# Transposes of rotated q and k, of the softmax and of the gated q and k: squares of 32 on VectorE and GpSimd transfers in place of TensorE

## The chip, the cores and the metric

The kernel runs on one core of a Trainium2 chip. The metric is the device time of one execution in microseconds (us), smaller is better. The time before is 1736.4 us, the median of three runs (1735.93 to 1738.6).

## The reference

One decoder layer on a sequence of 256 tokens of width 2048, in float32: a gated feed-forward block (FFN), a mixer of two kinds of attention, and a second FFN. Cut to what matters here:

```
x = x + 0.5 * swiglu(rms_norm(x, g1), w_gate1, w_up1, w_down1)
h = rms_norm(x, g_mix)
q_g, k_g, v_g, g_low, r_g, q_a, k_a, v_a = split(h @ w_in)
# group A: gated linear attention, 4 heads, chunks of 64 positions
b = cumsum(log_a) per chunk           # log_a from g_low
o_g = intra(q_g*exp(b-b_ref), k_g*exp(b_ref-b), v_g) + inter(q_g*exp(b), k_g*exp(b_last-b), v_g)
# group B: dilated attention, 8 heads of 128
qa, ka = rope(rms_norm(q_a)), rope(rms_norm(k_a))
o_a = softmax over three dilated causal windows (qa ka^T) v_a
x = x + concat(rms_norm(o_g) * silu(r_g), o_a) @ w_out
x = x + 0.5 * swiglu(rms_norm(x, g2), w_gate2, w_up2, w_down2)
```

## The kernel before, in words

Tokens lie on partitions in two tiles of 128 (t = 0, 1; `NT` is 2). Every large product is made of float32r matmuls of 128x512 on TensorE. To keep float32 accuracy a weight tile is split into a high part `wh` (ScalarE, L113) and a low part `wl` (VectorE, L114), and three products are added up: high by high (L274), low by high (L276), high by low (L278). A weight tile is 128x1024, and serves 12 such matmuls. `wh` and `wl` have four buffers each (`WBUF`), so the two engines that split can run a few tiles ahead of TensorE and no more.

`column_pair` makes 1024 columns of one projection: 16 weight tiles, for both token tiles, then an evacuation from PSUM by ScalarE (`store` for q, k, v). The mixer runs the pairs in the order q, k, v of the dilated attention, the low-rank gate (`gate_low`, 32 matmuls of 128x256, two weight tiles whose free columns GpSimd clears at L203), q and k of the linear attention (`qg`, `kg`), its v, its output gate, and then the output projection. The small work of the attention itself is put into the list `later` as closures, and each pair runs that list off between its own products: head work of q is done while k's products run, and so on. Tile then schedules all instructions with its own model of the engines, and that decides in which order each engine gets them. An engine works through its queue strictly in this order.

What the change touches:

- `rotate` (L596) normalizes and rotates 128x512 of q or k (four heads) on VectorE into `m1`; four TensorE transposes (L109) put it into a PSUM bank, and ScalarE copies that into `qT` or `kT` (L610). It runs 8 times.
- `scores` (L639) makes the scores of one head from `qT` and `kT` (L642) in a bank from `tp_bank`, adds the mask (L645), takes the softmax (L649 to L654) into `sc`. `values` (L657) transposes three blocks of `sc` on TensorE, copies them to `pT` on ScalarE (L663), and multiplies with v (L666 to L668) into another bank; `split` writes the output as `oah` (ScalarE) and `oal` (VectorE). 8 heads each.
- `scaled` (L730) transposes `qg` and `kg`, 128x512 per token tile, on TensorE, and VectorE multiplies the bank with the decays `e1`, `e2`, `e3` (L736).
- `tp_bank` (L80) has two banks only, taken in rotation by transposes, scores, values and the small products of the linear attention.
- `squares` (L126) and `move_squares` (L130) are there already, and the FFN uses them: one VectorE instruction transposes each square of 32x32 in place of its own, and 16 GpSimd transfers then carry the squares to the partitions where they belong. All GpSimd transfers go through one queue in order, with GpSimd's other work.

Of the kernel before, what the change touches and what calls it, by code (L numbers as in the profile page):

```python
# [14 lines left out]
F32 = mybir.dt.float32  # L15
# [33 lines left out]
def layer_kernel(tc, x, xT, gains, gla_gate_up, gla_gate_bias, gla_out_norm, att_q_norm, att_k_norm,  # L49
# [6 lines left out]
    with ExitStack() as es:  # L56
# [69 lines left out]
        def squares(dst, src):  # L126

            nc.vector.transpose(dst.rearrange("p (q j c) -> p j q c", q=4, j=4), src)

        def move_squares(dst, src):  # L130
            for q in range(4):
                for r in range(4):
                    nc.gpsimd.dma_start(dst[32 * q:32 * q + 32, r * P:(r + 1) * P], src[32 * r:32 * r + 32, q * P:(q + 1) * P])  # L133
# [406 lines left out]
        with tc.tile_pool(name="mix", bufs=1, reuse_waits="tile") as mp:  # L540
# [55 lines left out]
            def rotate(i, dst, t, half, xn):  # L596
                rs = head_scale(xn, 4, HD)
# [9 lines left out]
                tb = tp_bank()  # L607
                for h in range(4):
                    transpose(tb[:, h * P:(h + 1) * P], m1[:, h * P:(h + 1) * P])
                nc.scalar.activation(dst[:, 4 * half:4 * half + 4, t * P:(t + 1) * P], v(tb), AF.Copy)  # L610

            def store(dst, after=None):

                def f(t, ps):
                    for j in range(2):
                        blk = dst[:, t, j * 512:(j + 1) * 512]
                        nc.scalar.activation(halves(blk), ps[j], AF.Copy, scale=rt[:, t:t + 1])
                        if after:
                            later.append(lambda blk=blk, j=j: after(t, j, blk))
# [4 lines left out]


            xq, qT = big("xq"), big("qT")
            qTv = qT.rearrange("p (h s) -> p h s", h=AH)
            column_pair(hacts, store(tok(xq), lambda t, j, b: rotate(0, qTv, t, j, b)), span=14, due=8)
            xk, kT = big("xk"), big("kT")
            kTv = kT.rearrange("p (h s) -> p h s", h=AH)  # L630
            column_pair(hacts, store(tok(xk), lambda t, j, b: rotate(1, kTv, t, j, b)))
# [7 lines left out]
            def scores(h):  # L639
                b = tp_bank()  # L640
                for t in range(NT):
                    nc.tensor.matmul(b[:, t * P:t * P + (t + 1) * P], lhsT=qTv[:, h, t * P:(t + 1) * P],  # L642
                                     rhs=kTv[:, h, :(t + 1) * P], start=True, stop=True)
# [11 lines left out]
                heads[h] = sc  # L655

            def values(h):  # L657
                sc = heads.pop(h)
                tb = tp_bank()
                for j in range(3):  # L660
                    transpose(tb[:, j * P:(j + 1) * P], sc[:, j * P:(j + 1) * P])
                pT = mp.tile([P, 3 * P], F32, name="pT", tag="sc", bufs=6)
                nc.scalar.activation(pT, tb[:, :3 * P], AF.Copy)  # L663
                ob = tp_bank()
                v0, v1 = (vav[:, t, h * HD:(h + 1) * HD] for t in range(NT))
                nc.tensor.matmul(ob[:, 0:P], lhsT=v0, rhs=pT[:, 0:P], start=True, stop=True)  # L666
                nc.tensor.matmul(ob[:, P:S], lhsT=v0, rhs=pT[:, P:2 * P], start=True, stop=False)
# [9 lines left out]
            for h in range(0, AH, 2):  # L677
                later.append(lambda h=h: both(scores, h))
                if h:
                    later.append(lambda h=h: both(values, h - 2))  # L680
# [235 lines left out]
```

## Time and profile before

| | us |
|---|---|
| median of 3 runs | 1736.4 |
| the profiled execution | 1736.26 |
| its span in the trace | 1734.5 |
| TensorE (PE) busy | 1725.2 |
| VectorE (DVE) busy | 1299.5 |
| ScalarE (ACT) busy | 921.3 |
| GpSimd (POOL) busy | 438.9 |

The profile is of one execution. Its span is 1.8 us shorter than the time of the same execution, and that time is 0.14 us below the median. "Busy" counts an instruction from its start to its end; instructions of one engine overlap at their ends, so the distance between two starts is shorter than a duration. Times in the text count from the start of the span.

### The profile page before, as it was taken

The page shows a single profiled execution, that of the slowest core. Times are in us where ns is not written, and L with a number is a line of the kernel's source. Part 1 is how long each engine was busy: PE and PEld are TensorE (multiplying, and loading weights), DVE is VectorE, ACT ScalarE, POOL GpSimd, SP SyncE. Part 2 cuts the span into 40 slices and gives each one's busy share as a digit, 9 for nine tenths or more (in the row PEclk, how much of TensorE's full clock was granted, in tenths as well). Part 3 has the DMA queues.
Part 4 walks back from the last instruction along what each step waited for, and adds up shares of the span by engine and source line. Part 5 has one row for each costly group of instructions (what it writes and reads, how often), then busy time and mean ns, then how long its engine had stood idle before and what let it go on. Part 6 is the DMA issues. An engine that isn't in the chain of part 4 may idle for free.

```text
span 1734.5 us, 22127 instructions
## 1 busy us (share of the span) xinstructions
PE 1725.2 (99%) x8100; PEld 1503.4 (87%) x8100; DVE 1299.5 (75%) x1535; ACT 921.3 (53%) x1142; POOL 438.9 (25%) x870
## 2 busy tenths in 40 slices
PE   9999999999999999999999999999999999999999
PEld 7888888888888888888888888888888888888887
DVE  7788888855788787566655658688888965687875
ACT  7555555544555554565754545455555544455453
POOL 0333334444300601011000033333333343320000
PEclk9999999999999999999999999999999999999999
DMA  8666566666656656555444465556666666655653
GB/s 341 219 221 228 207 215 224 234 221 220 209 201 222 209 216 241 194 195 210 161 170 161 155 207 186 226 209 234 224 225 223 219 216 223 209 211 210 232 213 137
DMA packets 80846, 367.59 MB, mean 212 GB/s; under 512 B 19249, under 2 KB 36657, under 8 KB 38497
## 3 DMA queue, kind: packets, MB, share of 16 engines
q1 hardware_dynamic: 50864, 350.25, 55.9%
q0 software_dynamic: 29152, 14.87, 3.4%
q8 instruction: 63, 1.03, 0.2%
q10 hardware_dynamic: 720, 1.07, 0.2%
q14 instruction: 47, 0.38, 0.1%
HBM read 350.38 MB, written 2.10 MB: 203 GB/s over the span
## 4 chain that ended last, share of the span: by engine, by line
PE 82%; DVE 9%; DMA 5%; issue 2%; ACT 1%; POOL 1%; SPq 0%; DVEq 0%; ACTq 0%
PE acc L276 20%; PE acc L278 20%; PE acc L274 20%; DVE wl L114 4%; DMA raw<-in_w_ff_dram 4%; PE tp L278 3%; PE tp L276 3%; PE tp L274 3%; PE acc L300 2%; PE acc L299 2%; PE acc L298 2%; ACT wh L113 1%; DVE raw L246 1%; DMA urs<-us 1%; DVE t L238 1%
## 5 line engine op out<-in xcount | busy, mean ns | idle before, releaser
L114 DVE TENSOR_TENSOR wl<-raw,wh 128x1024 fp32r<-128x1024 f32 (+1 forms) x658 | 793.3, 1218 | 302.9 <-ACT wh L113 299.4
L113 ACT ACTIVATE wh<-raw 128x1024 fp32r<-128x1024 f32 (+1 forms) x660 | 682.2, 1048 | 562.5 <-PE acc L278 337.0
L133 POOL DMA_DIRECT2D urs<-us x704 | 344.3, 497 | 551.9 <-issue 287.6
L276 PE MATMUL acc<-wl,hh 128*128 128x512 f32 x1376 | 416.6, 381 | 0.4 <-DVE wl L114 0.4
L278 PE MATMUL acc<-wh,hl 128*128 128x512 f32 x1376 | 414.6, 380 | 0.0
L274 PE MATMUL acc<-wh,hh 128*128 128x512 f32 x1376 | 409.2, 381 | 1.6 <-ACT wh L113 1.6
L274 PEld LDWEIGHTS acc<-wh,hh 128*128 128x128 f32 x1376 | 259.5, 189 | 39.3 <-ACT wh L113 2.7
L276 PEld LDWEIGHTS acc<-wl,hh 128*128 128x128 f32 x1376 | 259.4, 189 | 38.6 <-DVE wl L114 1.5
L278 PEld LDWEIGHTS acc<-wh,hl 128*128 128x128 f32 x1376 | 259.6, 189 | 36.5
L276 PE MATMUL acc<-wl,uh 128*128 128x512 f32 x408 | 122.8, 379 | 0.0
L278 PE MATMUL acc<-wh,ul 128*128 128x512 f32 x408 | 122.5, 379 | 0.0
L274 PE MATMUL acc<-wh,uh 128*128 128x512 f32 x408 | 119.6, 379 | 0.2 <-ACT wh L113 0.2
L133 POOL DMA_DIRECT2D hh<-us x128 | 62.2, 508 | 158.9 <-issue 133.5
L274 PEld LDWEIGHTS acc<-wh,uh 128*128 128x128 f32 x408 | 77.0, 189 | 11.6 <-ACT wh L113 0.6
L278 PEld LDWEIGHTS acc<-wh,ul 128*128 128x128 f32 x408 | 77.1, 189 | 11.0
L276 PEld LDWEIGHTS acc<-wl,uh 128*128 128x128 f32 x408 | 77.1, 189 | 10.9
L165 POOL TENSOR_TENSOR rs<-a,mhalf 128x4 f32<-128x4 f32 (+1 forms) x12 | 17.4, 1454 | 256.8 <-DVE a L592 256.8
L274 PE MATMUL tp<-wh,hh 128*128 128x512 f32 x192 | 58.6, 379 | 0.0
L278 PE MATMUL tp<-wh,hl 128*128 128x512 f32 x192 | 57.1, 379 | 0.0
L276 PE MATMUL tp<-wl,hh 128*128 128x512 f32 x192 | 57.1, 379 | 0.0
L238 DVE TENSOR_TENSOR t<-raw 128x1024 f32<-128x1024 f32 x28 | 33.8, 1207 | 25.6 <-DMA raw<-in_w_ff_dram 25.6
L113 ACT ACTIVATE wh<-t 128x1024 fp32r<-128x1024 f32 x28 | 29.5, 1054 | 39.7 <-DVE t L238 33.0
(273 smaller groups left out, 1994.8 us busy)
## 6 DMA issues: line engine op xcount, KB each, us to landing
raw<-in_w_ff_dram SPq DMA_DIRECT2D x175, 1024.0 KB, 5.0
raw<-in_w_dn_dram SPq DMA_DIRECT2D x88, 1024.0 KB, 4.8
raw<-in_w_mix_dram SPq DMA_DIRECT2D x48, 1024.0 KB, 4.7
raw<-in_w_out_dram SPq DMA_DIRECT2D x16, 1024.0 KB, 4.8
urs<-us POOLq DMA_DIRECT2D x704, 16.0 KB, 3.6
xs<-in_x_dram SPq DMA_DIRECT2D x2, 1024.0 KB, 9.7
hh<-us POOLq DMA_DIRECT2D x128, 16.0 KB, 3.4
xt<-in_xT_dram SPq DMA_DIRECT2D x7, 256.0 KB, 6.6
```

The source lines that it names most:

```text
L113: nc.scalar.activation(dst_h, src, AF.Copy)
L114: nc.vector.tensor_sub(dst_l, src, dst_h.bitcast(F32))
L133: nc.gpsimd.dma_start(dst[32 * q:32 * q + 32, r * P:(r + 1) * P], src[32 * r:32 * r + 32, q * P:(q + 1) * P])
L165: nc.gpsimd.tensor_tensor(dst, src, mhalf[:, :src.shape[-1]], op=ALU.pow)
L238: nc.vector.tensor_add(room["sum"], b1, mid)
L246: nc.vector.tensor_add(raw[:, 1, j, :], b, raw[:, 1, j, :])
L274: nc.tensor.matmul(ps[j], lhsT=sh, rhs=alt(wh[:, j, :]), start=first and i == 0, stop=False)
L276: nc.tensor.matmul(ps[j], lhsT=sh, rhs=alt(wl[:, j, :]), start=False, stop=False)
L278: nc.tensor.matmul(ps[j], lhsT=sl, rhs=alt(wh[:, j, :]), start=False, stop=last and i == len(ws) - 1)
L298: nc.tensor.matmul(bank, lhsT=a[0], rhs=alt(ws[0][:, j, :]), start=start, stop=False)
L299: nc.tensor.matmul(bank, lhsT=a[0], rhs=alt(ws[1][:, j, :]), start=False, stop=False)
L300: nc.tensor.matmul(bank, lhsT=a[1], rhs=alt(ws[0][:, j, :]), start=False, stop=stop)
```

## The change

Three groups of TensorE transposes go. In their place come `squares` on VectorE and `move_squares` on GpSimd, which now also moves two blocks at a time (32 partitions, two runs of 128 or of 96 elements). ScalarE's copies out of PSUM behind the transposes go with them; for q there are copies from SBUF instead, which put the heads' columns in order; k and the softmax are read in the order of squares by TensorE. `rotate` is cut in two: the heads' scales are queued first (`head_scale`), the rotations behind them (`turned`), so that GpSimd's small powers don't stand behind its transfers. The list `later` gets empty steps between a move and its use. Buffers that are free at the time (`qg`, `kg`, `la`, `e123`) hold the squares on their way.

```diff
-        def squares(dst, src):
-            nc.vector.transpose(dst.rearrange("p (q j c) -> p j q c", q=4, j=4), src)
+        def squares(dst, src, j=4):
+            nc.vector.transpose(dst.rearrange("p (q j c) -> p j q c", q=4, j=j), src)

         def move_squares(dst, src):
+            n = dst.shape[-1] // 4
             for q in range(4):
                 for r in range(4):
-                    nc.gpsimd.dma_start(dst[32 * q:32 * q + 32, r * P:(r + 1) * P], src[32 * r:32 * r + 32, q * P:(q + 1) * P])
+                    nc.gpsimd.dma_start(dst[32 * q:32 * q + 32, ..., r * n:(r + 1) * n], src[32 * r:32 * r + 32, ..., q * n:(q + 1) * n])
...
-            def rotate(i, dst, t, half, xn):
-                rs = head_scale(xn, 4, HD)
+            def rotate(i, dst, t, half, xn, rs):
...
-                tb = tp_bank()
-                for h in range(4):
-                    transpose(tb[:, h * P:(h + 1) * P], m1[:, h * P:(h + 1) * P])
-                nc.scalar.activation(dst[:, 4 * half:4 * half + 4, t * P:(t + 1) * P], v(tb), AF.Copy)
+                stage = (qg, kg)[t] if i == 0 else (la, e123[:, 2])[t]
+                squares(stage[:, half, :], m1)
+                if half:
+                    move_squares(dst[:, :, t, :], stage)
+                    if i == 0:
+                        for b in range(2):
+                            copied.append(lambda b=b: nc.scalar.activation(
+                                runs(qTv[:, 4 * b:4 * b + 4, t * P:(t + 1) * P]), in_order(dst[:, b, t, :]), AF.Copy))
...
-                            later.append(lambda blk=blk, j=j: after(t, j, blk))
+                            scales = []
+                            later.append(lambda blk=blk, scales=scales: scales.append(head_scale(blk, 4, HD)))
+                            turned.append(lambda blk=blk, j=j, scales=scales: after(t, j, blk, scales[0]))
+                    if after and t:
+                        for f in turned:
+                            later.extend([f, lambda: None])
+                        later.extend([lambda: None] * 5 + [lambda: copied and copied.pop(0)()] * 4)
+                        turned.clear()
...
             def scores(h):
-                                     rhs=kTv[:, h, :(t + 1) * P], start=True, stop=True)
+                                     rhs=head_runs(kTv, h, t + 1), start=True, stop=True)
...
-                heads[h] = sc
+                us = (qg, kg)[h // 2 % 2].rearrange("p t f -> p (t f)")[:, h % 2 * 3 * P:(h % 2 + 1) * 3 * P]
+                squares(us, sc, 3)
+                if h % 2:
+                    both_us = (qg, kg)[h // 2 % 2].rearrange("p t f -> p (t f)")[:, :6 * P].rearrange("p (h f) -> p h f", h=2)
+                    move_squares(pTs[:, h - 1:h + 1, :], both_us)

             def values(h):
-                for j in range(3):
-                    transpose(tb[:, j * P:(j + 1) * P], sc[:, j * P:(j + 1) * P])
-                pT = mp.tile([P, 3 * P], F32, name="pT", tag="sc", bufs=6)
-                nc.scalar.activation(pT, tb[:, :3 * P], AF.Copy)
+                pT = pTs[:, h, :].rearrange("p (q j c) -> p j q c", q=4, j=3)
...
                 later.append(lambda h=h: both(scores, h))
-                if h:
-                    later.append(lambda h=h: both(values, h - 2))
-            later.append(lambda: both(values, AH - 2))
+                later.append(lambda: None)
+                if h > 2:
+                    later.append(lambda h=h: both(values, h - 4))
+            for h in (AH - 4, AH - 2):
+                later.extend([lambda: None, lambda h=h: both(values, h)])
...
             def scaled(t):
-                for src, dsts in ((qg, (e1, e3)), (kg, (e2,))):
-                    tb = tp_bank()
-                    for h in range(GH):
-                        transpose(tb[:, h * P:(h + 1) * P], src[:, t, h * P:(h + 1) * P])
+                for i, dsts in ((0, (e1, e3)), (1, (e2,))):
                     for d in dsts:
-                        nc.vector.tensor_mul(d[:, t, :], tb, d[:, t, :])
+                        d = runs(d[:, t, :].rearrange("p (j q) -> p j q", j=4))
+                        nc.vector.tensor_mul(d, in_order(moved[:, t, i, :]), d)
...
+            def turn_qk(t):
+                for i, a in enumerate((qg, kg)):
+                    squares(turn[:, t, i, :], a[:, t, :])
+                move_squares(moved[:, t], turn[:, t])
...
-            for f in (decays, scaled, intra):
+            for f, n in ((turn_qk, 0), (decays, 0), (scaled, 2), (intra, 0)):
                 for t in range(NT):
-                    later.append(lambda f=f, t=t: f(t))
+                    later.extend([lambda: None] * n + [lambda f=f, t=t: f(t)])
```

The scheduler's order moves at two places. In the rows below a name carries its buffer's number, and lines of the changed kernel are 2 or more higher: L276, L278 and L280 are the three products, L722 and L723 the gate's, L672 the scores', L695 to L697 the values'.

**First place: TensorE and ScalarE where the pair of v ends.** `va` is v, and its banks are acc_6499 to acc_6508 before, acc_6480 to acc_6498 after. TensorE before:

```order
L276 MATMUL acc_6508<-wl_6742,hh_79 128x512
L278 MATMUL acc_6507<-wh_6741,hl_80 128x512
L278 MATMUL acc_6508<-wh_6741,hl_80 128x512
L695 MATMUL acc_6802<-hh_79,wh_6759 128x256
L696 MATMUL acc_6802<-hl_80,wh_6759 128x256
```

TensorE after:

```order
L280 MATMUL acc_6497<-wh_6773,hl_80 128x512
L280 MATMUL acc_6498<-wh_6773,hl_80 128x512
L276 MATMUL acc_6956<-wh_6831,hh_79 128x512
L278 MATMUL acc_6956<-wl_6832,hh_79 128x512
L280 MATMUL acc_6956<-wh_6831,hl_80 128x512
L276 MATMUL acc_6956<-wh_6851,hh_79 128x512
L278 MATMUL acc_6956<-wl_6852,hh_79 128x512
L280 MATMUL acc_6956<-wh_6851,hl_80 128x512
L722 MATMUL acc_6828<-hh_79,wh_6791 128x256
```

Six products of the next pair (`acc_6956`) have moved in between the last product of v and the gate. ScalarE at the same place, before:

```order
L113 ACTIVATE wh_6759<-raw_6757 128x8x16
L113 ACTIVATE wh_6763<-raw_6757 128x8x16
L113 ACTIVATE wh_6805<-raw_6803 128x1024
L617 ACTIVATE va_6470<-acc_6499,rt_75 128x512
L617 ACTIVATE va_6470<-acc_6500,rt_75 128x512
L617 ACTIVATE va_6470<-acc_6507,rt_75 128x512
L617 ACTIVATE va_6470<-acc_6508,rt_75 128x512
L113 ACTIVATE wh_6825<-raw_6803 128x1024
```

And after:

```order
L113 ACTIVATE wh_6773<-raw_6755 128x1024
L624 ACTIVATE va_6464<-acc_6480,rt_75 128x512
L624 ACTIVATE va_6464<-acc_6481,rt_75 128x512
L624 ACTIVATE va_6464<-acc_6497,rt_75 128x512
L624 ACTIVATE va_6464<-acc_6498,rt_75 128x512
L113 ACTIVATE wh_6831<-raw_6829 128x1024
L113 ACTIVATE wh_6851<-raw_6829 128x1024
L113 ACTIVATE wh_6791<-raw_6789 128x8x16
L113 ACTIVATE wh_6795<-raw_6789 128x8x16
```

The gate's two tiles (128x8x16) and the next pair's first tile stood ahead of the four evacuations of v; now all of them stand behind. GpSimd's queue at this place, after (`kT<-la` and `kT<-e` are the moves of k's two token tiles, `e_5745` the tile e123; before there was none of the moves, and the two clearings of `wh` stood right behind those of `sm`):

```order
L135 DMA kT<-la_5744 32x2x128 x16
L797 MEMSET sm 128x512
L725 DMA gbias<-in_gla_gate_bias_dram 128x512
L797 MEMSET sm 128x512
L135 DMA kT<-e_5745 32x2x128 x16
L205 MEMSET wh 128x1024 x2
```

The clearing of the gate's tiles now stands behind 32 transfers.

**Second place: TensorE and VectorE at the last heads' scores.** `tp_7255` before is the bank of a head's values; after, tp_7195 and tp_7211 are the scores of heads 6 and 7, tp_7277 and tp_7283 the values of heads 2 and 3, tp_7329 and tp_7335 those of heads 4 and 5. TensorE before, around one head's values:

```order
L278 MATMUL acc_7384<-wh_7418,hl_80 128x512
L278 MATMUL acc_7385<-wh_7418,hl_80 128x512
L666 MATMUL tp_7255<-pT_7253,va_6470 128x128
L667 MATMUL tp_7255<-pT_7253,va_6470 128x128
L668 MATMUL tp_7255<-pT_7253,va_6470 128x128
L109 MATMUL tp_7261<-ident_70,sc_7081 128x128 x3
L274 MATMUL acc_7392<-wh_7418,hh_79 128x512
L274 MATMUL acc_7393<-wh_7418,hh_79 128x512
```

TensorE after:

```order
L672 MATMUL tp_7195<-kT_6079,qT_5747 128x128
L672 MATMUL tp_7195<-kT_6079,qT_5747 128x256
L672 MATMUL tp_7211<-kT_6079,qT_5747 128x128
L672 MATMUL tp_7211<-kT_6079,qT_5747 128x256
L695 MATMUL tp_7277<-e123_5745,va_6464 128x128
L696 MATMUL tp_7277<-e123_5745,va_6464 128x128
L697 MATMUL tp_7277<-e123_5745,va_6464 128x128
L695 MATMUL tp_7283<-e123_5745,va_6464 128x128
L696 MATMUL tp_7283<-e123_5745,va_6464 128x128
L697 MATMUL tp_7283<-e123_5745,va_6464 128x128
L695 MATMUL tp_7329<-e123_5745,va_6464 128x128
L696 MATMUL tp_7329<-e123_5745,va_6464 128x128
```

Small products stood singly between large ones; now two heads' scores and four heads' values follow each other with no large product between. VectorE after, behind the mask addition of head 6 (`sc_7198`):

```order
L679 TENSOR_REDUCE nm_7200<-sc_7198 128x1 x2
L675 TENSOR_TENSOR sc_7214<-tp_7211,bm_5726 128x384
L681 RECIPROCAL li_7202<-l_7201 128x2
L679 TENSOR_REDUCE nm_7216<-sc_7214 128x1 x2
L684 TENSOR_SCALAR sc_7198<-sc_7198,li_7202 128x128
L684 TENSOR_SCALAR sc_7198<-sc_7198,li_7202 128x256
L128 STREAM_TRANSPOSE kg_5743<-sc_7198 128x3x4x32
L681 RECIPROCAL li_7218<-l_7217 128x2
L684 TENSOR_SCALAR sc_7214<-sc_7214,li_7218 128x128
L684 TENSOR_SCALAR sc_7214<-sc_7214,li_7218 128x256
L128 STREAM_TRANSPOSE kg_5743<-sc_7214 128x3x4x32
L114 TENSOR_TENSOR oal_5724<-tp_7277,oah_5723 128x256
```

The reading of a values' bank (`oal`) stands behind the whole softmax of two heads, where before it stood between splits of weights. Up to the mixer all engines keep their order.

28 lines of the change are left out of this document (17 added, 11 removed).

## The prediction

> **What bounds the kernel now.** I read the page's busy times first, then the windows by stage, then the waits.
>
> ```profile
> span 1734.5 us, 22127 instructions
> PE 1725.2 (99%) x8100; PEld 1503.4 (87%) x8100; DVE 1299.5 (75%) x1535; ACT 921.3 (53%) x1142; POOL 438.9 (25%) x870
> core 0: us, PE busy (x) PEld busy (x) DVE busy (x) ACT busy (x) POOL busy (x), PEclk, DMA share, GB/s
> 722.00:764.00 42.00, 42.00 (x204) 36.82 (x203) 28.86 (x40) 25.48 (x56) 7.44 (x4) 1.00 0.53 196
> 764.00:809.00 45.00, 45.00 (x218) 39.44 (x217) 28.91 (x41) 26.84 (x59) 10.68 (x9) 1.00 0.57 209
> 809.00:863.00 54.00, 54.00 (x282) 47.47 (x281) 36.56 (x64) 37.73 (x62) 0.00 (x0) 1.00 0.49 175
> 863.00:925.00 62.00, 62.00 (x331) 54.72 (x330) 36.23 (x51) 34.85 (x53) 0.00 (x0) 1.00 0.46 159
> ```
>
> TensorE is busy in 1725.2 of 1734.5 us. The four windows cover the stages that the change touches (k's products with q's rotation; v's with k's; the gate and the scores; the linear attention's v), and in each TensorE is busy all the time at a granted clock of 1.00. So every piece of its work there is worth its full length, and every wait that the change makes on TensorE is lost for good: no idle time exists to take it. VectorE and ScalarE are free for a third of these stages, GpSimd nearly always.
>
> **Term 1, the transposes that go.** The groups by form give their number, the timeline what four of them cost.
>
> ```profile
> L109 PE MATMUL tp<-ident,m 128*128 128x128 f32 x32 | 4.8, 273 | 0.0
> L109 PE MATMUL tp<-ident,sc 128*128 128x128 f32 x24 | 3.9, 273 | 0.0
> L109 PE MATMUL tp<-ident,qg 128*128 128x128 f32 x8 | 1.2, 273 | 0.0
> L109 PE MATMUL tp<-ident,kg 128*128 128x128 f32 x8 | 1.2, 273 | 0.0
> ...
> 736.65 0.38 PE L278 MATMUL acc<-wh,hl 128*128 128x512 f32 x1
> 736.87 0.60 PE L109 MATMUL tp<-ident,m 128*128 128x128 f32 x4
> 737.23 0.46 PE L278 MATMUL acc<-wh,hl 128*128 128x512 f32 x1
> 737.52 0.38 PE L274 MATMUL acc<-wh,hh 128*128 128x512 f32 x1
> ...
> 738.60 0.59 PE L274 MATMUL acc<-wh,hh 128*128 128x512 f32 x2
> 739.03 0.59 PE L276 MATMUL acc<-wl,hh 128*128 128x512 f32 x2
> ```
>
> Two products take 739.03 - 738.60 = 0.43 us from start to start. From 736.65 to 737.52 there are two products and four transposes in 0.87 us, so four transposes take 0.44, one 0.11. All 32 + 24 + 8 + 8 = 72 go: 72 x 0.109 = **-7.85 us**. The 273 ns of a row is a latency, most of which lies beside the next instruction.
>
> [...] The distance of the starts decides here.
>
> **Edits that cost nothing.** VectorE gets 8 + 4 squares of 128x512 at 710 ns and 8 of 128x384, near the 551 of the mask addition (rows below): 8.5 + 4.4 = 12.9 us in 203 us of windows, of which it is busy 130.6. ScalarE loses 16 copies out of PSUM and gets 4. The four copies for q wait for transfers at the head of ScalarE's queue, with splits of weights behind them; but nine splits stand there between the last of q's head scales and the first copies, each paced by 12 products (2.6 us): 23 us, for one move of some 8 us to issue and 4 to land (term 4). If that cover went, each microsecond past it would cost TensorE one. The products of decays read the moved squares later still. Scores and values read runs of 32 where they read 128; the products already read two interleaved halves at 0.216 us, so I put that at nothing, with ends of 0 and +2 us (24 values' and 16 scores' rhs, 0.05 each).
>
> **Term 2, TensorE waits where v ends.** In the new order the first tile of the next pair (`wh_6831`) is split behind the four evacuations of v, and TensorE wants it right after v's last product. Before, 32 gate products lay there, with tiles that were ready.
>
> ```profile
> 807.71 2.56 ACT L617 ACTIVATE va<-acc,rt 128x512 f32<-128x512 f32 x4
> ...
> 809.02 0.29 PE L695 MATMUL acc<-hh,wh 128*128 128x256 f32 x1
> ...
> L113 ACT ACTIVATE wh<-raw 128x1024 fp32r<-128x1024 f32 x654 | 679.0, 1053 | 554.1 <-PE acc L278 337.0 <-PE tp L278 75.3 <-DVE raw L246 69.4
> L114 DVE TENSOR_TENSOR wl<-raw,wh 128x1024 fp32r<-128x1024 f32 x654 | 790.6, 1222 | 298.8 <-ACT wh L113 295.3
> ```
>
> The evacuations ended at 810.27, 1.25 us after v's last product, because the last two wait for it. With 1.05 for the split TensorE idles 2.3 us. It then has one product (0.22) before it wants `wl_6832`, which takes 1.22 more: 1.0 idle. Then two products before `wl_6852`, another 1.22 behind: 0.5 idle. Together **+3.8 us**; bounds 0, if ScalarE or the products run ahead of what the order lets me see, and 4.5.
>
> **Term 3, TensorE waits at heads 2 to 7.** Scores of heads 6 and 7 and values of heads 2 to 5 follow each other on TensorE. There are two `tp` banks; head 4's values need the bank of head 2's values, whose last reader (`oal`) stands on VectorE behind the softmax of heads 6 and 7.
>
> ```profile
> 853.96 0.82 PE L642 MATMUL tp<-kT,qT 128*128 128x128 f32 x4
> 854.61 0.49 PE L109 MATMUL tp<-ident,sc 128*128 128x128 f32 x3
> 859.69 0.38 PE L666 MATMUL tp<-pT,va 128*128 128x128 f32 x2
> 860.36 0.49 PE L109 MATMUL tp<-ident,sc 128*128 128x128 f32 x3
> ...
> L645 DVE TENSOR_TENSOR sc<-tp,bm 128x384 f32<-128x384 f32 x8 | 4.4, 551 | 0.6 <-PE tp L642 0.6
> 867.86 0.61 DVE L649 TENSOR_REDUCE nm<-sc 128x1 f32<-128x128 f32 x2
> 870.99 0.55 DVE L654 TENSOR_SCALAR sc<-sc,li 128x128 f32<-128x128 f32 x2
> L128 DVE STREAM_TRANSPOSE us<-u 128x512 f32<-128x512 f32 x44 | 31.2, 710 | 1.0
> L114 DVE TENSOR_TENSOR oal<-tp,oah 128x256 fp32r<-128x256 f32 x8 | 3.4, 420 | 0.2 <-ACT oah L113 0.2
> ...
> L650 ACT ACTIVATE sc<-sc,nm 128x256 f32<-128x256 f32 x8 | 3.9, 493 | 0.0
> L650 ACT ACTIVATE sc<-sc,nm 128x128 f32<-128x128 f32 x8 | 3.2, 398 | 6.4 <-DVE nm L649 6.4
> ```
>
> One head's scores take 854.61 - 853.96 = 0.65 us of TensorE, one head's values 0.67. From the end of head 6's scores VectorE needs, one after the other: addition 0.55, reductions 0.61 and head 7's addition 0.5 (the exponentials, 0.4 + 0.5 and their sums, run meanwhile on ScalarE and end at about 1.9), reciprocal 0.1, reductions 0.6, scaling 0.55, squares 0.55, and for head 7, whose exponentials end by then, 0.1, 0.55 and 0.55; then `oal` 0.42. That is 5.3 us. TensorE fills 0.65 + 0.67 + 0.67, less 0.2 of latency: 1.8. So it idles **+3.5 us**; bounds 1.5 (half the small instructions overlapping) and 5.
>
> I add **+0.5** for the third scores of the stage, which need a bank whose mask addition now stands behind the gate's logarithms (bounds 0 and 1).
>
> **Term 4, GpSimd's queue.** It gets 10 moves of 16 transfers. No row shows a transfer of 64 runs; the rows nearest are these, by runs: 32, 128, and 256 after a pause. The last row is the landing of the 32.
>
> ```profile
> L133 POOL DMA_DIRECT2D urs<-us x704 | 344.3, 497 | 551.9 <-issue 287.6 <-ACT sg L425 123.3 <-DMA urs<-us 62.8
> L564 POOL DMA_DIRECT2D bm<-in_c_mask_dram x1 | 0.5, 547 | 0.0
> L560 POOL DMA_DIRECT2D rope<-in_c_rope_dram x1 | 0.8, 752 | 40.1 <-PE tp L300 40.1
> L203 POOL MEMSET wh<- 128x1024 f32 x2 | 1.9, 953 | 11.2 <-PE acc L278 11.2
> ...
> 797.36 1.23 DVE L114 TENSOR_TENSOR wl<-raw,wh 128x1024 fp32r<-128x1024 f32 x1 [1.80 <-ACT wh L113]
> ...
> DMA to landing us min/median/max: 1.6/3.6/7.1
> ```
>
> I take 0.52 an issue, near the 0.497. Behind k's two moves stand the two clearings of the gate's tiles, and TensorE waits for these. k's last squares follow the split that started at 797.36 before: 797.36 + 1.23 - 3.5 (32 transposes less ahead) + 0.7 = 795.8, or 798.2 if k's four squares at 0.6 push everything on VectorE. Sixteen issues (8.3), two clearings (1.9) and the small splits (about 0.8) end at 806.8 to 809.2. v now ends at 809.0 - 3.5 = 805.5, and the gate comes 3.8 of waiting and 6 products (1.3) later, at 810.6. So **0**, with 1.4 to 3.8 us to spare. The values' moves take 8.3 + 3.6 from their squares; heads 4 and 5 need theirs at about the time that term 3 frees the bank, so this hides in term 3.
>
> **Sum**, against the profiled execution's own 1736.26: 1736.26 - 7.85 + 3.8 + 3.5 + 0.5 = **1736.2 us**. The median of the runs is 0.14 above that execution, which changes nothing. The work leaves TensorE, and nearly the same time comes back as waits of its own queue.
>
> **The rivals.**
>
> *The waits are smaller.* The list of waits has this for all of TensorE's waits on ScalarE's `wh` for L274 (total, times, longest):
>
> ```profile
> PE acc L274 <- ACT wh L113: 1.9, 2, 1.6
> ```
>
> For it: a longest wait of 1.6 us, though evacuations and splits meet at every pair's end. Against it: nothing stands in TensorE's queue that could fill these two. With both gone it is 1736.26 - 7.85 = 1728.4; with one gone 1732.5. Chance 0.22.
>
> *GpSimd's queue decides (the other side).* At an issue above about 0.6 us the clearings come after TensorE wants the gate: 32 x 0.08 = 2.6 uses up the spare time. At the 0.752 of rope's row the clearings come 4 to 8 us later, less the spare: about +6; and the moves of heads 2 to 5, which queue behind each other, come some 9 late, of which the bank hides 3: +6. That is 1748. For it: twice the runs in each transfer, and three dimensions as rope has. Against it: 128 runs took 0.547. Chance 0.18 (1740 to 1749). [...]
>
> *The landing decides.* If a move lands nearer 7.1 than 3.6 us after issue, values of heads 2 to 5 wait past the bank: +3.5 at most, 1739.7. Chance 0.1, half of it beyond 0.2%.
>
> *The transposes were no full cost*, or the reads in runs of 32 slow the small products: 1738 to 1740. Against it: the row of starts. Chance 0.05.
>
> *The forecast* has the rest, 0.45.
>
> **How the numbers follow.** 0.2% is 3.5 us, about what a measurement of this kernel can tell from no change. Faster than 1732.9: the rival with small waits and the forecast's lower tail, 0.24. Slower than 1739.9: GpSimd's queue and half the landing, 0.25. Within: 0.51. The range leaves a tenth out on each side: low 1730.5 (waits of 2 us in all), high 1745 (an issue of about 0.68).
>
> **What would show it.** The L109 groups of m, sc, qg and kg are gone, and TensorE's waits name ScalarE's `wh` with some 2.3 us and VectorE's `wl` with 1.5 near 806, VectorE's `oal` with about 3 near 870. GpSimd's L135 rows should read about 0.52 us. A wait of the gate on GpSimd's clearing means the second rival; waits of the values on a transfer, the third. A span below 1730 without those waits means that the order was no guide to the time.

## The result and the profile after

| | before | after |
|---|---|---|
| median of 6 runs each, side by side | 1736.16 us (1735.56 to 1738.6) | 1744.79 us (1743.74 to 1749.95) |
| ratio of the times | | 1.0052, 95% interval 1.0041 to 1.0063 |
| span of the profiled execution | 1734.5 us | 1742.8 us |

The change makes the kernel slower by 0.5%. The prediction was 1736.2 us: no change.

First the head of the changed kernel's page, to set beside the same lines of before.

```profile
span 1742.8 us, 22221 instructions
PE 1724.5 (99%) x8028; PEld 1501.0 (86%) x8028; DVE 1308.8 (75%) x1555; ACT 915.2 (53%) x1130; POOL 521.5 (30%) x1030
```

TensorE has 72 instructions fewer, as it should, but its busy time fell by 0.7 us only, where 7.85 were to go, and the span grew by 8.3. Idle time alone can't do that: some busy time must have become slower. The windows of 10 us show where (columns as in the windows of before: busy us of each engine, then the granted clock, the DMA share and GB/s).

```profile
core 0: us, PE busy (x) PEld busy (x) DVE busy (x) ACT busy (x) POOL busy (x), PEclk, DMA share, GB/s
800.00:810.00 10.00, 7.14 (x30) 5.26 (x29) 2.35 (x2) 4.42 (x6) 9.63 (x19) 0.97 0.51 181
810.00:820.00 10.00, 9.34 (x46) 8.22 (x46) 2.24 (x5) 2.42 (x4) 2.11 (x3) 0.69 0.58 216
...
870.00:880.00 10.00, 5.02 (x29) 4.14 (x28) 5.29 (x17) 3.36 (x12) 9.26 (x19) 0.88 0.30 102
880.00:890.00 10.00, 10.00 (x43) 8.83 (x42) 4.23 (x6) 4.48 (x7) 6.27 (x12) 0.78 0.14 36
```

TensorE idles at two places here (a short third idle, near 837 us, is in the list below), and behind both the granted clock is below 1 (0.69 and 0.78 in the rows behind them). The last row is the instructive one: TensorE is busy for all of its 10 us and does 22% less. The four clocks below 1 stand for (0.03 + 0.31 + 0.12 + 0.22) x 10 = 6.8 us of lost clock, which no list of waits contains. Not all of it is lost work, since a slow clock costs nothing while TensorE idles anyway. The slow stretches last from 809.35 to 816.18 and from 877.62 to 884.45 us at a clock of 0.50; these are their first halves:

```profile
809.35:812.77 3.42, 2.76 (x9) 1.46 (x8) 1.24 (x3) 0.62 (x2) 2.76 (x4) 0.50 0.58 177
...
877.62:881.03 3.41, 1.73 (x8) 1.76 (x9) 1.16 (x2) 1.34 (x3) 3.41 (x8) 0.50 0.18 48
```

TensorE was idle there for 0.66 and 1.68 us, and busy in both second halves throughout. Half of the 11.3 busy us is lost to the clock, 5.7 us. The idle itself is in the list of TensorE's waits (total us, times, longest):

```profile
PE tp L695 <- DMA e<-qg: 5.0, 2, 4.8
PE acc L276 <- ACT wh L113: 3.9, 3, 2.1
...
PE acc L278 <- DVE wl L114: 1.2, 3, 0.8
PE tp L672 <- DVE sc L675: 0.7, 1, 0.7
PE acc L722 <- DVE wh L114: 0.7, 1, 0.7
```

In the stages of the change these are 4.97 at the values (L695), 2.08 and 0.78 where v ends, 0.66 at the gate (L722) and 0.68 at the third scores (L672), together 9.2. The balance: -7.85 + 9.2 + 5.7 = +7.0 us, against +8.3 of the spans. Of the 1.3 us that it lacks, about 0.6 are transposes that were worth a little less than their price (e9 below); the rest is not explained.

The timeline of TensorE at the first place, then of GpSimd there (start, duration, engine, line, in brackets the idle ahead and what ended it):

```profile
807.67 0.48 PE L276 MATMUL acc<-wh,hh 128*128 128x512 f32 x1 [2.08 <-ACT wh L113]
808.93 0.48 PE L278 MATMUL acc<-wl,hh 128*128 128x512 f32 x1 [0.78 <-DVE wl L114]
...
811.95 0.58 PE L722 MATMUL acc<-hh,wh 128*128 128x256 f32 x1 [0.66 <-DVE wh L114]
...
813.18 0.41 PE L723 MATMUL acc<-hl,wh 128*128 128x256 f32 x1
813.40 0.41 PE L722 MATMUL acc<-hh,wh 128*128 128x256 f32 x1
```

```profile
799.96 0.54 POOL L797 MEMSET sm<- 128x512 f32 x1
800.43 0.58 POOL L725 DMA_DIRECT2D gbias<-in_gla_gate_bias_dram  x1
801.00 0.54 POOL L797 MEMSET sm<- 128x512 f32 x1
801.47 2.65 POOL L135 DMA_DIRECT2D kT<-e  x5
804.48 5.78 POOL L135 DMA_DIRECT2D kT<-e  x11 [0.37 <-DMA kT<-la]
810.26 1.86 POOL L205 MEMSET wh<- 128x1024 f32 x2
```

The waits at `wh` and `wl` stand where the prediction put the first two of its three. Behind them the gate's products start every 0.22 us (813.18 to 813.40); from 817.15 on, with the slow stretch over, they start every 0.12. The clearings of the gate's tiles, which the prediction had done by 809.2, begin at 810.26 only: the end of k's first move (its issues ran from 788.99 to 799.96, with 2.5 us of pauses for landings), two other clearings and the load of the gate's bias stand ahead of them in GpSimd's queue.

The second place, on TensorE, VectorE and GpSimd:

```profile
874.16 0.39 PE L697 MATMUL tp<-e,va 128*128 128x128 f32 x2
879.30 0.77 PE L695 MATMUL tp<-e,va 128*128 128x128 f32 x2 [4.75 <-DMA e<-qg]
...
882.84 0.64 PE L280 MATMUL acc<-wh,hl 128*128 128x512 f32 x1
883.27 0.63 PE L276 MATMUL acc<-wh,hh 128*128 128x512 f32 x1
```

```profile
861.76 1.03 DVE L128 STREAM_TRANSPOSE qg<-sc 128x384 f32<-128x384 f32 x2
...
876.73 0.72 DVE L114 TENSOR_TENSOR oal<-tp,oah 128x256 fp32r<-128x256 f32 x2
```

```profile
868.65 3.16 POOL L135 DMA_DIRECT2D e<-qg  x6
872.54 5.32 POOL L135 DMA_DIRECT2D e<-qg  x10 [0.74 <-DMA e<-kg]
```

The squares of heads 4 and 5 were ready at 862.8. Their 16 transfers were issued from 868.65 to 877.86, because those of heads 2 and 3 stood ahead, and GpSimd itself waits, between issues, for landings of earlier transfers. From the first transfer of heads 0 and 1 (847.75) to the last of heads 4 and 5 these pauses add up to 4.7 us, the 48 issues to 25.4. The bank that the prediction let the values wait for was free at 877.45; the last transfer had landed 1.9 us later, when the values began; its issue had ended 1.4 us before that. Behind this idle too the products start every 0.43 us (882.84 to 883.27), twice the usual 0.216.

So three things were to be shown: that the low clock comes from the idle and not from something else that the change brings; how much idle it takes; and what holds the values.

### The profile page after: what moved, and what is told of

It is laid out like the page before. It is cut to its first block, busy times and chain, and to the rows that moved or that the text cites. A ratio compares the mean times of both kernels' runs of the same rounds, so it can differ in the third digit from the quotient of the medians.

```text
span 1742.8 us, 22221 instructions
## 1 busy us (share of the span) xinstructions
PE 1724.5 (99%) x8028; PEld 1501.0 (86%) x8028; DVE 1308.8 (75%) x1555; ACT 915.2 (53%) x1130; POOL 521.5 (30%) x1030
## 4 chain that ended last, share of the span: by engine, by line
PE 85%; DVE 6%; DMA 4%; issue 2%; ACT 1%; POOL 1%; SPq 0%; DVEq 0%; ACTq 0%; POOLq 0%
PE acc L278 21%; PE acc L280 21%; PE acc L276 20%; PE tp L278 4%; PE tp L280 4%; PE tp L276 4%; PE acc L302 3%; PE acc L301 3%; PE acc L300 3%; DVE wl L114 2%; DMA raw<-in_w_ff_dram 2%; PE tp L300 1%; PE tp L302 1%; PE tp L301 1%; ACT wh L113 1%
## 5 line engine op out<-in xcount | busy, mean ns | idle before, releaser
L278 PE MATMUL acc<-wl,hh 128*128 128x512 f32 x1376 | 417.2, 381 | 1.3 <-DVE wl L114 1.2
L280 PE MATMUL acc<-wh,hl 128*128 128x512 f32 x1376 | 415.9, 381 | 0.0
L276 PE MATMUL acc<-wh,hh 128*128 128x512 f32 x1376 | 408.9, 382 | 4.0 <-ACT wh L113 3.6
L276 PEld LDWEIGHTS acc<-wh,hh 128*128 128x128 f32 x1376 | 260.6, 190 | 42.5 <-ACT wh L113 5.0
L278 PEld LDWEIGHTS acc<-wl,hh 128*128 128x128 f32 x1376 | 260.2, 190 | 40.6 <-DVE wl L114 4.0
L280 PEld LDWEIGHTS acc<-wh,hl 128*128 128x128 f32 x1376 | 260.6, 190 | 37.2 <-issue 0.5
L278 PE MATMUL acc<-wl,uh 128*128 128x512 f32 x408 | 122.9, 379 | 0.0
L280 PE MATMUL acc<-wh,ul 128*128 128x512 f32 x408 | 122.6, 379 | 0.0
L276 PE MATMUL acc<-wh,uh 128*128 128x512 f32 x408 | 119.7, 379 | 0.2 <-ACT wh L113 0.2
L276 PEld LDWEIGHTS acc<-wh,uh 128*128 128x128 f32 x408 | 77.1, 189 | 11.5 <-ACT wh L113 0.7
L278 PEld LDWEIGHTS acc<-wl,uh 128*128 128x128 f32 x408 | 77.2, 189 | 10.9
L280 PEld LDWEIGHTS acc<-wh,ul 128*128 128x128 f32 x408 | 77.2, 189 | 10.9
L276 PE MATMUL tp<-wh,hh 128*128 128x512 f32 x192 | 58.6, 379 | 0.0
L278 PE MATMUL tp<-wl,hh 128*128 128x512 f32 x192 | 57.1, 379 | 0.0
L280 PE MATMUL tp<-wh,hl 128*128 128x512 f32 x192 | 57.1, 379 | 0.0
```

The costliest lines, as they stand in the source:

```text
L276: nc.tensor.matmul(ps[j], lhsT=sh, rhs=alt(wh[:, j, :]), start=first and i == 0, stop=False)
L278: nc.tensor.matmul(ps[j], lhsT=sh, rhs=alt(wl[:, j, :]), start=False, stop=False)
L280: nc.tensor.matmul(ps[j], lhsT=sl, rhs=alt(wh[:, j, :]), start=False, stop=last and i == len(ws) - 1)
```

## The experiments

Theory 1: an idle of TensorE costs its length and a stretch at half the clock behind it. Rival A: the clock falls for the change's reads in runs of 32 or its transfers. Theory 2: the values wait because moves queue on GpSimd. Rival C: the bank or the landing holds them. Times are medians, ratios are to the kernel before in the same comparison.

**The gate's clearings on VectorE** (e1).

```diff
-                    nc.gpsimd.memset(w.bitcast(F32), 0.0)
+                    nc.vector.memset(w.bitcast(F32), 0.0)
```

> The changed kernel, but the two clearings of the gate's tiles run on VectorE, so the gate's tiles no longer stand behind k's moves in GpSimd's queue, and the gate's products come right behind v's again, as they did before the change. Theory 1 (each longer idle of TensorE costs its own length and a stretch at about half the granted clock behind it): the idle near 806 to 812 goes (3.5 us) and the slow rows there too (0.3 + 3.1 us by the 10-us windows), so 1744.8 - 3.5 - 3.4 = 1737.9. Rival A (the low clock comes from what the change adds, small products that read in runs of 32 and the traffic of the moves, not from the idle): the idle goes and the clock row near 815 stays at about 0.7, 1741.3. Both hold only if the second idle, near 875, stays as it is.

Measured: 1739.66 us, ratio 1.0018 (1.0009 to 1.0027). The time lies between the two theories, since the second idle did not stay: it grew from 4.97 to 7.9. The windows decide:

```profile
810.00:820.00 10.00, 10.00 (x44) 8.04 (x43) 6.69 (x9) 5.54 (x6) 2.88 (x6) 1.00 0.71 260
860.00:870.00 10.00, 5.99 (x41) 5.16 (x39) 5.91 (x18) 3.40 (x12) 8.84 (x18) 1.00 0.40 144
870.00:880.00 10.00, 6.12 (x25) 5.63 (x26) 2.15 (x4) 2.03 (x4) 10.00 (x20) 0.66 0.19 49
```

With the first idle its slow window is gone (1.00 where it was 0.69), with all the moves and reads of the change in place; only the idle at the values still has one. That speaks for theory 1. TensorE and VectorE at the values in this kernel:

```profile
866.33 0.39 PE L696 MATMUL tp<-e,va 128*128 128x128 f32 x2
...
867.00 0.39 PE L696 MATMUL tp<-e,va 128*128 128x128 f32 x2
...
873.88 0.77 PE L695 MATMUL tp<-e,va 128*128 128x128 f32 x2 [6.27 <-DMA e<-qg]
```

```profile
868.74 0.71 DVE L114 TENSOR_TENSOR oal<-tp,oah 128x256 fp32r<-128x256 f32 x2
```

The bank was free at 869.45, 4.4 us before the values began: here the transfers alone set their start, which speaks against rival C's bank. GpSimd issued the last of these transfers until 872.46, 1.4 us before the values: the landing was short, and the queue held them. From head to head (866.33 to 867.00) the values take 0.67 us, as before the change: the reads in runs of 32 cost nothing.

**The softmax by TensorE again** (e2): in the changed kernel, scores and values as before the change.

```diff
-                squares(us, sc, 3)
...
-                    move_squares(pTs[:, h - 1:h + 1, :], both_us)
+                heads[h] = sc
...
-                pT = pTs[:, h, :].rearrange("p (q j c) -> p j q c", q=4, j=3)
...
+                for j in range(3):
+                    transpose(tb[:, j * P:(j + 1) * P], sc[:, j * P:(j + 1) * P])
...
+                nc.scalar.activation(pT, tb[:, :3 * P], AF.Copy)
...
```

> The changed kernel with the softmax as before the change (24 transposes on TensorE, 8 copies on ScalarE, values one step behind their scores); rotated q and k and the gated q and k still go by squares. Theory 1: the idle near 875 goes (4.8 us), the slow rows at 870 to 890 too (1.2 + 2.2 us), 24 transposes come back (2.6 us): 1744.8 - 4.8 - 3.4 + 2.6 = 1739.2; the first idle and its slow row stay. Rival A (the clock drops for the squares' reads or the transfers): 1742.6 or more. Rival B (the scores' reads of k in runs of 32 cost TensorE): scores still take longer than 0.65 us a head.

Measured: 1739.2 us, ratio 1.0016 (1.0007 to 1.0025), as theory 1 had it. The windows from 860 to 890 are full at a clock of 1.00; the first idle stays (a wait of 2.08 again), with its slow window:

```profile
810.00:820.00 10.00, 8.82 (x42) 7.47 (x41) 2.26 (x4) 1.68 (x3) 2.75 (x4) 0.66 0.60 221
```

The scores of a head, which still read k in runs of 32, take 0.47 or 0.66 us of TensorE from their first start to the next product's, as they do before the change, so rival B falls.

**Both edits** (e3).

> Both edits together: clearings on VectorE and the softmax by TensorE. It has 48 transposes fewer than the kernel before (5.2 us). Theory 1: no idle of over 1 us is left in the stages of the change, the granted clock is 1.00 in every window, and the time is 1736.2 - 5.2 = 1731.0, less than both kernels. Rival A (clock drops without the idles): some 3 to 7 us more, 1734 to 1738.

Measured: 1732.24 us, ratio 0.9972 (0.9962 to 0.9983), faster than both kernels. Each window from 800 to 890 has TensorE busy for 10.00 at 1.00. Without idles the price of a transpose can be read. These are VectorE's last evacuations ahead of the mixing stage and behind it, of the kernel before and then of this one:

```profile
679.86 0.68 DVE L483 SCALAR_TENSOR_TENSOR xs<-acc,xs 128x512 f32<-128x512 f32 x1
...
1058.01 1.88 DVE L832 TENSOR_TENSOR xs<-xs,acc 128x512 f32<-128x512 f32 x3
```

```profile
682.27 0.68 DVE L485 SCALAR_TENSOR_TENSOR xs<-acc,xs 128x512 f32<-128x512 f32 x1
...
1055.14 1.88 DVE L864 TENSOR_TENSOR xs<-xs,acc 128x512 f32<-128x512 f32 x3
```

The stage takes 378.15 us before and 372.87 here: 5.28 less for 48 transposes, 0.110 each. In the changed kernel the same distance is 8.1 more than before.

**Idles put into the kernel before** (g1): at six places of the feed-forward a tiny product, a chain of n powers on GpSimd, a tiny product that reads its result, and all later products behind it.

```diff
...
+            tc.keep_in_program_order(nc.tensor.matmul(b[:8, :8], lhsT=mhalf, rhs=mhalf, start=True, stop=True))
+            nc.vector.tensor_copy(x[:8], b[:8, :8])
+            for _ in range(n):
+                nc.gpsimd.tensor_tensor(x[:8], x[:8], mhalf[:8], op=ALU.pow)
+            last = nc.tensor.matmul(b[:8, :8], lhsT=x[:8], rhs=x[:8], start=True, stop=True)
+            tc.keep_in_program_order(last)
...
+            pins[0].enter_context(tc.issue_after(last.ins))
```

> The kernel before with six idles of TensorE put into plain stretches of the feed-forward products, of about 0.5, 1, 2 and then 1, 6 and 4 us (a tiny product waits for a chain of 0, 1, 2, 1, 5 and 3 powers on GpSimd that starts from another tiny product; all later products stand behind it). Nothing else of the change is in it. Theory 1: behind the idles of 2 us and more the products start every 0.43 us instead of 0.216 for some 3 to 6 us (2 to 3.4 us lost each), behind those under 1 us they don't; the clock rows dip at these places alone. Theory 1b (the stretch grows with the idle): the 6 us idle is followed by about three times the slow stretch of the 2 us one. Rival A: the clock is 1.00 throughout, and the time is the kernel before plus the sum of the idles.

Measured: 1770.28 us in one execution. The idles came out as 0.24, 2.00, 3.77, 2.00, 8.89 and 5.48 us. The two of the same length differ:

```profile
408.47 0.20 PE L375 MATMUL tp<-x 8*8 8x8 f32 x2 [2.00 <-POOL x L374]
...
409.13 0.59 PE L276 MATMUL acc<-wl,hh 128*128 128x512 f32 x2
409.56 0.59 PE L278 MATMUL acc<-wh,hl 128*128 128x512 f32 x2
...
1427.96 0.20 PE L375 MATMUL tp<-x 8*8 8x8 f32 x2 [2.00 <-POOL x L374]
...
1429.10 1.06 PE L276 MATMUL acc<-wl,hh 128*128 128x512 f32 x2
1429.95 1.06 PE L278 MATMUL acc<-wh,hl 128*128 128x512 f32 x2
```

A pair of products takes 0.43 us behind the first and 0.85 behind the second. Nothing of the change is in this kernel, so here the idle alone, without the change, lowered the clock. Nor does the slow stretch grow in proportion to the idle (theory 1b): 3.4 us behind 3.77, 3.3 behind 5.48, 5.6 behind 8.89. The ends of the slow stretches, 458.7, 1431.5, 1486.1 and 1533.9 (each placed within its pair of products by the pair's duration), are 285, 16 and 14 times 3.413 us apart.

**Equal idles** (g2): the same device with one power at nine places and two at nine.

> The kernel before with 18 idles of TensorE in the plain feed-forward stretches: nine of about 2.0 us near 350 to 460, nine of about 3.8 us near 1420 to 1550. In the run with six idles, one of 2.00 us had no slow stretch behind it and another of 2.00 us had one of 3.4 us; the slow stretches ended at 458.7, 1431.4, 1485.9 and 1533.9 us, whose distances are 285.0, 16.0 and 14.1 times 3.41 us. Theory 1c (the chip decides at the ends of fixed windows of 3.41 us that run on regardless of the program, and a window with enough idle makes the next one slow): all slow stretches begin and end on one grid of 3.41 us; of the 2.0 us idles those that lie nearly whole in one window are followed by a slow stretch, those that a window's end cuts in two are not; so some 3 to 6 of nine; of the 3.8 us idles nearly all. Theory 1 without a grid: equal idles have equal consequences, all nine or none.

Measured: 1808.92 us in one execution. At six of the 18 places other products slipped in and the idle was 0.4 us or less. Six idles of 2.0 and six of 3.77 us are left.

```profile
411.47 0.20 PE L375 MATMUL tp<-x 8*8 8x8 f32 x2 [2.06 <-POOL x L374]
...
413.59 1.06 PE L274 MATMUL acc<-wh,hh 128*128 128x512 f32 x2
...
415.98 0.59 PE L274 MATMUL acc<-wh,hh 128*128 128x512 f32 x2
...
420.89 0.20 PE L375 MATMUL tp<-x 8*8 8x8 f32 x2 [2.02 <-POOL x L374]
...
421.55 0.59 PE L276 MATMUL acc<-wl,hh 128*128 128x512 f32 x2
```

The slow stretches behind the idles end at 374.84, 415.80, 1443.22, 1456.87, 1501.24, 1511.47, 1555.86 and 1566.09, all on one grid: 12, 313, 317, 330, 333, 346 and 349 times 3.4133 us behind the first. The period is read from these ends: 40.96 us between the first two and 1191.25 between the first and the last, 12 and 349 periods. On this grid two of the 2.0 us idles lie whole in one window (that of 411.47 is one), and the next window ran at half speed (a pair of products in 0.85 us instead of 0.43); four are cut by a window's end, and no slow stretch followed. The largest part of an idle in one window without a slow one behind it was about 1.7 of 3.41 us, the smallest with one 2.03. Waits within one window added up at one place: a ninth slow stretch, 1613.88 to 1617.29 (the granted clock from 1610 to 1620 is 0.83), lies behind two waits of the feed-forward's own that put 1.17 and 0.75 us into the window ahead of it, 1.93 together. All six of 3.77 were followed by one slow window or two. Fewer of the short ones had a slow window than the 3 to 6 of nine expected; the grid itself is as theory 1c has it.

**Half of the softmax's transfers issued by SP** (e5), with the clearings on VectorE and all 72 transposes gone.

```diff
-                    move_squares(pTs[:, h - 1:h + 1, :], both_us)
+                    for q in range(4):
+                        for r in range(4):
+                            (nc.gpsimd if r % 2 else nc.sync).dma_start(
+                                pTs[32 * q:32 * q + 32, h - 1:h + 1, 96 * r:96 * r + 96],
+                                both_us[32 * r:32 * r + 32, :, 96 * q:96 * q + 96])
```

> The changed kernel with the clearings on VectorE (as in the first experiment) and, of each of the four moves of the softmax, 8 of the 16 transfers issued by SP instead of GpSimd; all 72 transposes stay away from TensorE. Theory 2 (the values wait for their transfers because the moves of four pairs of heads, 16 x 0.535 = 8.6 us each, stand behind each other in GpSimd's queue): the idle at L695 falls from 7.9 us to under 1, and with it its slow stretch goes, so 1736.0 - 7.85 + 1 = about 1729. Rival C (the bank, whose reader stands behind the softmax on VectorE, or the landing itself, holds the values): the idle stays at 3.5 us or more, with a slow stretch, 1733 to 1737. Rival D (SP's issues for the moves wait for the squares and hold back loads of weights behind them): TensorE waits for a split or a load instead, 1732 or more.

Measured: 1734.1 us, ratio 0.9981 (0.9972 to 0.999). The idle at the values is gone, as theory 2 has it: no wait for a transfer is in TensorE's list, and the windows at 860 and 870 have a clock of 1.00. The time is 5 us above the 1729 expected, for a new wait at another place, which leads the list:

```profile
PE tp L109 <- DVE hf L123: 3.7, 1, 3.7
```

Near 1070 the second feed-forward's first transposes wait for VectorE, and VectorE for the last move of the normalised input; the window behind has a clock of 0.83, worth 1.7 us at most. 3.7 + 1.7 = 5.4 is about what is missing.

**The same by ScalarE** (e6, `nc.scalar` for `nc.sync`).

> The same, with ScalarE in SP's place as the issuer of half the transfers. Theory 2: as with SP, about 1729, unless ScalarE, which splits the weights, stands waiting for the squares at its queue's head; each microsecond of that beyond what the weight tiles hold ready costs TensorE one: 1729 to 1733. Rival C: 1733 to 1737.

Measured: 1741.7 us, ratio 1.0031 (1.002 to 1.0042). TensorE's waits for ScalarE's splits grow to 4.9 us, the wait near 1070 is there too with 3.5, and four windows between 860 and 1090 have a clock of 0.81 to 0.94. ScalarE, whose splits TensorE waits for, was no place for transfers that wait: 1741.7 us against 1734.1 with SP.

**SP's help alone** (e8): the edit of e5 in the changed kernel, the clearings left on GpSimd.

> The changed kernel with one edit, half of the softmax's transfers issued by SP; the clearings of the gate's tiles stay on GpSimd. Theory 2 (the values wait because moves queue behind each other on GpSimd): the first idle (806 to 812) with its slow windows stays, the second (near 875) goes: 1744.8 - 4.8 - 3.4 = 1736.6, or up to 5 more if the wait near 1070 shows here too. Rival C (the bank or the landing holds the values): the second idle stays at 3 us or more, 1743 to 1745.

Measured: 1745.07 us, ratio 1.0044 (1.0032 to 1.0057). That is rival C's time, not theory 2's: the idle at the values fell to 2.7 us but did not go, and the wait near 1070 is there with 3.3.

```profile
848.33 4.28 POOL L691 DMA_DIRECT2D e<-qg  x8 [36.16 <-DVE kg L128]
858.69 0.76 PE L699 MATMUL tp<-e,va 128*128 128x128 f32 x2 [2.72 <-DMA e<-kg]
```

The values that wait are now the first ones, of heads 0 and 1. GpSimd had issued its half of their transfers by 852.61, SP its half by 850.80; the values began 6.1 us behind the later of the two, where it was 1.4 in e1. So it is the landing that holds them here, as one half of rival C has it, and no longer the queue. SP issued a load of weights right behind its half, at 850.90; that this load made the landings late is argued, not shown.

**The norms' moves too** (e7): half of the transfers of `norm_moved` by SP as well.

> The version with half of the softmax's transfers issued by SP, and now half of the transfers of the normalised input's moves too. In that version the idle at the values was gone, and a new wait of 3.7 us with a slow window (1.7 us) stood near 1070, where the second feed-forward's first transposes wait for VectorE, which waits for the last of the norm's moves on GpSimd. If this wait is the whole of what that version lost: 1734.1 - 3.7 - 1.7 = 1728.7, which is the kernel before less its 72 transposes (7.85). Rival D (SP's issues wait for squares and hold back loads of weights behind them): a split or a load is waited for near 690 or 1060, 1731 or more.

Measured: 1733.34 us, ratio 0.9983 (0.9974 to 0.9992). The wait near 1070 is gone. Rival D holds at the first norm, where loads stand behind SP's issues:

```profile
594.73 0.70 PE L280 MATMUL acc<-wh,uh 128*128 128x512 f32 x2 [3.53 <-ACT wh L113]
```

**Only the second norm's** (e9), beside e3 once more.

> As the version with SP's halves of the softmax's and the norms' transfers, but of the norms only the second, ahead of the second feed-forward. With both norms on SP the wait near 1070 was gone (TensorE busy 10.0 of 10 in each window there), and a wait of 3.5 us for a weight's split with a slow window stood near 594 instead, at the first norm, where loads stood behind SP's issues. If each of these is a matter of its own place: neither wait is left, all 72 transposes are gone, and the time is 1736.2 - 7.85 = 1728.4 to 1729.5. Rival D (SP's issues hold back loads at the second norm too): a split is waited for near 1060, 1731 or more.

> The version with the clearings on VectorE and the softmax by TensorE once more, on the same chip as the version above: 1732.2 as before, and 3 us above the other if that one has lost its waits.

Measured: 1730.06 us, ratio 0.9961 (0.9947 to 0.9974), and 1730.9 us, ratio 0.9973 (0.9963 to 0.9984). In e9 no wait at the values of over 0.3 us is left, and none near 594 or 1070. It has all reads and transfers of the change, and its mean granted clock is 1.000 (0.996 in the changed kernel): rival A falls. From the evacuation ahead of the mixing stage to the first one behind it e9 takes 369.4 us (680.12 to 1049.50), the kernel before 376.4 (679.86 to 1056.27). That is 7.0 less with 0.26 of waits, so the 72 transposes are worth 7.3 of the 7.85 us there; over the whole kernel the medians show 6.0. Both versions beat both kernels; the 3 us expected between them came out as 0.8, and e9 is not shown to beat e3, since their intervals overlap.

## Why the prediction was wrong

- **Term 1, the transposes** (-7.85): right for 48 of them, 0.110 us each in e3 where 0.109 was read from the starts; all 72 are worth 7.3 us in e9, so the softmax's 24 bring about 0.08 each.
- **Edits that cost nothing**: right. No wait for q's copies is in the list; the time of the values and of the scores is unchanged with runs of 32.
- **Term 2, where v ends** (+3.8): right in place and cause for two of its three waits, 2.08 + 0.78 = 2.9 us; the third, of 0.5, is not in the list. e1 and e3 show that it hangs on the gate's tiles: with these early, the gate's products fill the place again.
- **The third scores** (+0.5): 0.68.
- **Term 3, the values** (+3.5): 4.97, and the cause was not the bank. The bank alone would have held the values till 877.45, close to the prediction; the transfers held them till 879.3. e1, with the bank free 4.4 us earlier, shows the queue, and in e5, with half of the queue elsewhere, the idle is gone (though the scheduler has moved the values there).
- **Term 4, GpSimd's queue** (0): wrong by 0.66 at the gate and by what term 3 lacks. The issue was priced well (0.52 taken, 0.535 measured), but "with 1.4 to 3.8 us to spare" left out that other instructions stand between k's moves and the clearings, and that GpSimd waits for landings between issues. The same pauses, 4.7 us ahead of heads 4 and 5, and the moves of heads 2 and 3 made these transfers late: by an estimate from these numbers (879.3 less 4.7), without the pauses the last would have landed by about 874.6, ahead of the bank. The rival on the queue was right in its mechanism, at a smaller size and without its 0.6 us for an issue: 0.66 at the gate and 1.9 beyond the bank. That the measured time lies in its range (1740 to 1749) is luck, since the clock makes up the difference. The rival on the landing foresaw a wait for transfers, but the last one had landed within 2.0 us of the start of its issue, sooner than the 3.6 that the prediction took; slow landings did their harm through the pauses.
- **The step that failed** is the sentence on which every wait was priced: "every wait that the change makes on TensorE is lost for good". Each was counted at its length. The sum had no term for the clock behind an idle, which is 5.7 us of the 8.4 by which the profiled execution (1744.56) missed the forecast; the waits themselves, 9.2 against 7.8 foreseen, are 1.4 more, the transposes 0.6, and 0.7 is not explained.

The spread of the changed kernel's runs goes with the clock: its longest, 1749.95, had a mean clock of 0.994 where the others had 0.995 or 0.996. That the position of the idles on the grid makes this difference is argued, not shown.

Two things stay open: why GpSimd's norm moves near 1070 came late in e5, e6 and e8 and not in e3 (in the trace of e5 its queue stands for 3.25 us without a reason that the profile shows), and how values would wait with the queue free and the order of the changed kernel kept, since the scheduler moved them in e5.

## What to carry to other kernels

Work taken from a busy TensorE (99% of the span here) paid most in this case where no long idle appeared in return (e3 and e9, 0.9972 and 0.9961). In g2 an idle of which at most about 1.7 us lay in one window of 3.41 cost its length alone, one of 2.03 its length and up to 1.7 us more for the slow window behind it (half of 3.41, at a clock of 0.50); the idles of the changed kernel had two slow windows behind them each, and e8 had two behind waits of 1.48 us together in one window. So read the clock column behind every idle before pricing it. Before giving an engine's queue more transfers, list everything that already stands in it between the new ones and the instruction that TensorE waits for, and count the waits between issues. Where a queue is short by little, a second issuer can help, but only where nothing urgent stands behind it and the landing isn't what is waited for (e8): the same edit removed one wait near 1070 (3.7 us in e5) and made one near 594 (3.5 in e7).

## What the runs showed of the hardware

- In g2 the granted clock of TensorE changed on a grid of 3.413 us that was the same from 374.84 to 1617.29 us of the execution: an idle of about 1.7 us in a window left the next one at full speed, one of 2.03 halved it, and two waits of 1.93 together did so too. By these numbers an idle of 2 us cost 2.0 or up to 3.7 us, by where it fell. In the other traces, e1 idled for 1.83 us of a window (864.50 to 867.91) and kept its clock, e2 for 1.86 (807.24 to 810.65) and lost it. One window breaks this order: e8 lost its clock behind 1.48 us (807.04 to 810.46), with six products that stood among waits.
- Behind a slow window less idle was enough for another: one with 0.76 us of idle was followed by a slow one (g2 at 1450.8, slow till 1456.87), so was one with 0.66 (the changed kernel, 809.35), but not one with 0.35 (g2, 1562.68) or 0.42 (e5, 1071.12).
- In the changed kernel a GpSimd issue of a transfer of 64 runs took 0.535 us (0.534 to 0.539 by group), one of 32 runs 0.497. The transfers that write or read e123 there landed 1.7 to 5.7 us after their issue, 3.2 in the median.
